# Four groups of tiles instead of three, the first of a single tile, and four whole chunks instead of eight

## The chip, the cores and the metric

The kernel runs on one core of a Trainium2 chip. The metric is device time in microseconds (us) of one execution. Inputs and outputs lie in the chip's main memory; the engines are TensorE (matmul, PE in the rows), VectorE (DVE), ScalarE (ACT), GpSimd (POOL) and SyncE (SP, which here only issues transfers).

## The reference, cut to what matters

One layer of an encoder over 1024 prompt tokens and 64 sample tokens (which also see 512 cached positions). Two attention branches, a gated merge, and then a layer of experts, each a single neuron, chosen per token by product keys:

```python
h = rmsnorm(x, norm_mix);  z = h @ w_in          # 1024 -> 5536 columns
# branch A: differential attention, 8 heads; branch B: latent attention, 16 heads
merged = gates[:, :, 0] * (o_a @ w_branch_a) + gates[:, :, 1] * (o_b @ w_branch_b)
x = x + merged @ w_out
x = x + peer_ffn(rmsnorm(x, norm_ffn), ...)      # then a last rmsnorm

def peer_tokens(h, w_q, keys, u, v):             # 8 heads, 16 experts of 16384 each
    q = (h @ w_q).reshape(T, 8, 2, 64)
    s = einsum('thcd,hcnd->thcn', q, keys)
    ...                                          # two top-16, 256 candidates, top-16 again
    act = gelu(einsum('td,thkd->thk', h, u[idx]))
    return einsum('thk,thkd->td', g * act, v[idx])
```

All values are fp32. Attention is causal by chunks of 64, so a tile of 128 prompt tokens with number t attends to t + 1 tiles of keys.

## The kernel before, in words

The 1088 tokens are nine tiles: 0 to 7 of 128 prompt tokens, and 8 with the 64 sample tokens. `GROUPS` says which tiles go through the layer together; there are three groups of three. The loop over groups (line 576) does, for its tiles: norm and transposes; the projections by `w_in`; the difference attention; `w_a`; the latent attention (MLA); a unit is one head of one tile, 24 in the first attention of a group and 48 in the second; `w_b`, `w_out`, a second norm, `w_pq`, and the expert scores. Every group reads all weights again, in chunks of 1024 rows by 256 columns (1 MB). A *token-major* chunk (`tmajor`) has the tokens of one tile as the stationary operand and streams the 256 columns, 8 products a tile. A *channel-major* one (`cmajor`) has the weights as the stationary operand, two halves of 128 columns, and streams all tokens of the group (`NH` columns), 16 products whatever their width. Of 38 chunks 14 are token-major (`w_in` 0 to 9, `w_out`) and 24 channel-major.

The first group is not native: each fp32 operand is split into a high and a low part, and a product is three matmuls (`mm3`, lines 153 to 155). ScalarE makes the high part of a weight chunk and GpSimd the low one (`wload`, lines 178 and 179). Later groups are native: one fp32 product (line 167), which leaves two records.

After a group's scores, three kinds of background work are queued for each tile and are let into the instruction streams by `pump`, in a proportion that `spread` works out from the planned units of work and the dots left:

- `route_job` (queue r): the top-16 searches, on VectorE (lines 470 to 560).
- `dots_job` (queue d): 128 gathers of rows of `peer_u` by GpSimd's queue (line 333), one expert for each token of the tile, each with a dot product on VectorE (line 358); 64 gathers for the sample tile, which packs two experts. In the first part seven buffers hold gathered rows (four `gb`, three `gm`), in the passes the four `gb`.
- `build_job` (queue b): makes the tile's matrix of weights by expert from one-hot matrices on VectorE (lines 402, 403, 411), ScalarE (line 408) and small bf16 matmuls (line 418), and stores it in `Ad`.

So a group's gathers run beside the next group, and those of the last group beside the passes. The passes multiply the matrices by all of `peer_v`, 16 chunks of 1024 rows: pass 0 for tiles 0, 1, 2, pass 1 for 3, 4, 5, 6. The first `NWHOLE` chunks of pass 0 are whole fp32 (line 1206), all others split in three (line 1221), for which ScalarE and VectorE make high and low parts of `peer_v` (lines 1190, 1192) and of the matrix (1214, 1215). Tile 6 (`TR`) keeps part of its matrix in a buffer `Ares` that exists only from the passes on. The tiles of `VGATHER`, 7 and 8, have no matrix: `vgather_job` gathers rows of `peer_v` and adds them up with weights on VectorE (line 453).

A scheduler puts the recorded instructions of each engine into one fixed order; each engine then runs its own in that order and waits on semaphores.

Of the kernel before, what the change touches and what calls it, by code (L numbers as in the profile page):

```python
# [31 lines left out]
LAMBDA_INIT = 0.8 - 0.6 * math.exp(-0.3 * 0)  # L32
MAGIC = float(0x5F3759DF)
MSC = 96.0 ** -0.5
GROUPS = ((0, 1, 2), (3, 4, 5), (6, 7, 8))
PASSES = ((0, 1, 2), (3, 4, 5, 6))
VGATHER = (8, 7)
GN = 384
SLOT = 3072
NW = 3  # L40
# [1 line left out]
PB = 5  # L42
NB = 8
RC = 9
NWHOLE = 8
TR = 6
RATE_R2 = 0.41
RATE_B, RATE_B2 = 0.3, 0.5
PUMP_G = (1.1, 1.113, 1.158)
RATE_R_G = (0.7, 0.7, 0.623)  # L50
DEPTH_DIFF = (3, 2, 2)
DEPTH_MLA = (2, 2, 2)


def bcast_rows(ap1d, n):
# [4 lines left out]
def hybrid_tile(ctx: ExitStack, tc: tile.TileContext, A):  # L60
# [16 lines left out]
    neard = dram("neard", (H, 128, 2, 256), F32R)  # L77
    gateT = dram("gateT", (len(GROUPS), 16, 128, GN), F32)
    sd = dram("sd", (9, 128, 2, H, 128), F32)
# [34 lines left out]
    cur = {"gp": gp, "sm": sm, "ps": ps_mm, "more": None}  # L114
# [181 lines left out]
    def spread(units, dots):  # L296
        left["units"], left["dots"] = units, left["dots"] + dots
# [41 lines left out]
    def dots_job(t):  # L339
        if t in GROUPS[-1]:  # L340
            drain("r", ("route", t))
# [21 lines left out]
        ld(wgtd[t, :, :ns], wgt[:, :ns])  # L363
        if t not in VGATHER:
            queues["b"].append((("build", t), build_job(t)))

    def build_job(t):
        if t == TR:
            drain("r")
        src = bp.tile([128, 3, 128], F32, name="bsrc", tag="oh1")  # L370
        ld(src[:, 0, :], wgtd[t])
        ld(src[:, 1:3, :], efd[t])
        p = cur["ps"].tile([128, 512], F32, name="mm")
        pv = p.rearrange("p (a n) -> p a n", n=128)
        for i in range(3):
            PE.transpose(pv[:, i, :], src[:, i, :], ident)
        ixT = bp.tile([128, 2, 128], BF16, name="ixT")
        S.copy(ixT, pv[:, 1:3, :])
        aT = bp.tile([128, 128], F32, name="aT")
        S.copy(aT, pv[:, 0, :])  # L380
        a3 = bp.tile([128, 3, 128], BF16, name="a3")
        a3f = bp.tile([128, 128], F32, name="a3f")
        for i in range(3):
            V.tensor_copy(a3[:, i], aT)
            if i == 0:
                V.tensor_copy(a3f, a3[:, 0])
            if i < 2:
                V.tensor_tensor(aT, aT, a3[:, i], op=ALU.subtract)
        yield
        shp = [128, 4, 128, 2]  # L390
        iv = iota2[:, None, :, :].to_broadcast(shp)

        def over(row, tt):
            return row[:, tt:tt + 8].rearrange("p (g x) -> p g x", x=2)[:, :, None, :].to_broadcast(shp)

        n = RC if t == TR else 0
        for t0 in range(0, 128, 16):
            stage = bp.tile([128, 16, 4, 8, 4], F32, name="stage", tag="stage")
            for tt in range(t0, t0 + 16, 8):
                oh1 = bp.tile(shp, BF16, name="oh1", tag="oh1")  # L400
                oh2 = bp.tile(shp, BF16, name="oh2")
                V.tensor_tensor(oh1, iv, over(ixT[:, 1], tt), op=ALU.is_equal)  # L402
                V.tensor_tensor(oh2, iv, over(ixT[:, 0], tt), op=ALU.is_equal)  # L403
                w3 = bp.tile([128, 3] + shp[1:], BF16, name="w3")
                for i in range(3):
                    if i == 0:
                        for x in range(8):
                            S.activation(w3[:, 0, x // 2, :, x % 2], oh2[:, x // 2, :, x % 2], AF.Copy,  # L408
                                         scale=a3f[:, tt + x:tt + x + 1])
                    else:  # L410
                        V.tensor_tensor(w3[:, i], oh2, over(a3[:, i], tt), op=ALU.mult)
                for q in range(2):
                    p = cur["ps"].tile([128, 512], F32, name="mm")
                    pv = p.rearrange("p (a n) -> p a n", n=128)
                    for j in range(4):
                        x = 4 * q + j
                        for i in range(3):
                            PE.matmul(pv[:, j, :], lhsT=oh1[:, x // 2, :, x % 2], rhs=w3[:, i, x // 2, :, x % 2],  # L418
                                      start=i == 0, stop=i == 2)
                    pc = p.rearrange("p (t c i) -> p c i t", t=4, i=8)  # L420
                    if n:
                        S.copy(cur["Ares"][:, :, (tt + 4 * q) // 4], pc[:, :n])
                    if n < 16:
                        S.copy(stage[:, n:, (tt - t0) // 4 + q], pc[:, n:])
                    yield
            ld(Ad[t, :, n:, t0 // 4:t0 // 4 + 4], stage[:, n:])

    def finish(acc, nr, t):
        if t in VGATHER:
            y = gp.tile([128, D], F32, name="y", tag="gb")  # L430
# [5 lines left out]
    def vgather_job(t):  # L436
# [18 lines left out]
        if t == 8:  # L455
            oth = cur["gp"].tile([128, D], F32, name="gb", tag="gb")
            ld(oth[0:64], acc[64:128])
            V.tensor_tensor(acc[0:64], acc[0:64], oth[0:64], op=ALU.add)
        if t == VGATHER[-1]:
            cur["late"] = lambda: finish(acc, tr(t), t)  # L460
# [3 lines left out]
    def route_job(t, s_of):  # L464
# [100 lines left out]
        ld(gkd[t, :nr], gk[:nr].rearrange("p h k -> p (h k)"))  # L565
        if t not in VGATHER:
            queues["d"].append((("dots", t), dots_job(t)))
        elif t not in GROUPS[-1]:
            queues["d"].append((("dots", t), dots_job(t)))
        if t == max(x for x in GROUPS[-1] if x < 8):  # L570
            for v in [x for x in VGATHER if x in GROUPS[-1]]:
                queues["d"].append((("dots", v), dots_job(v)))
            for v in VGATHER:
                queues["d"].append((("vg", v), vgather_job(v)))

    for g, tiles in enumerate(GROUPS):
        cur["g"] = g
# [4 lines left out]
        if g:  # L582
            nbs = [t + 1 if t < 8 else 5 for t in tiles]
            spread(2.6 * 14 * len(tiles) + 3.9 * 2 * 24 + (H + MH) * sum(PUMP_G[g] * (1 + n * 0.5) for n in nbs),
                   128 * len(GROUPS[g - 1]))
# [189 lines left out]
        def diff_unit(t, h, Q, qc, K, Vt, nr_, L):  # L775
# [58 lines left out]
            pend.append(fin)  # L834
            flush(DEPTH_DIFF[g])

# [303 lines left out]
    Ares = p2.tile([128, RC, 32, 8, 4], F32, name="Ares", bufs=1)  # L1140
# [11 lines left out]
    cur["rp"], cur["rs"] = rpt, rst  # L1152
    cur["Ares"] = Ares
    rate["r"], rate["b"] = RATE_R2, RATE_B2
    spread(16 * 8 * 1.3 * sum(len(x) for x in PASSES), sum((128 if t < 8 else 64) for t in GROUPS[-1] + VGATHER))
    gfin = p2.tile([128, D], F32, name="gfin", bufs=1)
    ld(gfin, bcast_rows(A["norm_final"], D))
    cur["gfin"] = gfin
# [7 lines left out]
    for ip, tiles in enumerate(PASSES):  # L1166
# [11 lines left out]
        for c in range(16):  # L1178
            vb = []
            whole = ip == 0 and c < NWHOLE  # L1180
            for i in range(8):
# [12 lines left out]
            for t in tiles:  # L1194
# [21 lines left out]
                if t in pst:  # L1216
                    for i in range(8):
                        for L, R in ((ahi, vb[i][0]), (ahi, vb[i][1]), (alo, vb[i][0])):
                            for hf in range(2):
                                ds = slice(512 * hf, 512 * hf + 512)  # L1220
                                PE.matmul(pst[t][:, ds], lhsT=L[:, i, :], rhs=R[:, ds],  # L1221
                                          start=c == (0 if ip else NWHOLE and -1) and i == 0 and L is ahi and R is vb[i][0],
                                          stop=c == 15 and i == 7 and L is alo)
# [114 lines left out]
```

## Time and profile before

| | |
|---|---|
| runs, median of 3 | 4505.98 us (4502.06 to 4518.71) |
| profiled execution, whole | 4499.18 us |
| its span, first to last instruction | 4497.4 us |
| TensorE busy | 3847.6 us, 86% |
| VectorE busy | 3203.9 us, 71% |
| GpSimd busy | 1942.8 us, 43% |
| ScalarE busy | 1603.3 us, 36% |
| moved by DMA | 1183.10 MB, 263 GB/s on average |
| granted TensorE clock, mean | 0.892 |

A busy TensorE is not one at its peak: a record's length holds the pipeline, so the distance between the starts of neighbouring matmuls is the better price. The mean shares hide stages with different limits; the span is to be read by stages.

### The profile page before, as it was taken

To read this page: it belongs to the slowest core of one execution; us is meant where nothing else is said; L and a number is where in the kernel's file an instruction comes from. 1 tells how busy PE (TensorE), PEld (TensorE's weight loads), DVE (VectorE), ACT (ScalarE), POOL (GpSimd) and SP (SyncE) were. 2 spreads that over 40 slices of the span, in tenths; PEclk is the share of its full clock that TensorE was granted. 3 is DMA by queue.
4 is the path that set the end of the run, shared out by engine and by line. 5 is a ranking of instruction groups with operands and counts; after the bars stand their busy time and mean duration, and the time that the engine had idled before them with its cause. 6 is when DMAs were issued, how large, how long until landed. Compare 5 with 4: busy or idle time off the path is not lost.

```text
span 4497.4 us, 55226 instructions
## 1 busy us (share of the span) xinstructions
PE 3847.6 (86%) x18633; PEld 2898.2 (64%) x18633; DVE 3203.9 (71%) x7136; ACT 1603.3 (36%) x3656; POOL 1942.8 (43%) x1353
## 2 busy tenths in 40 slices
PE   6998988898788798887868877889999969999991
PEld 6977887556565565655546666654457858888881
DVE  4043457977788767797786777659847987777776
ACT  3344622025455513322454455133113532232320
POOL 3412241554456441143444656513434445545455
PEclk9967999987898898998778888989999979999995
DMA  5421244996777785697776767988868999989987
GB/s 176 168 96 56 67 170 169 352 350 231 267 263 269 272 320 216 226 329 290 245 248 239 256 239 253 351 291 311 320 246 317 349 328 332 351 312 352 321 314 260
DMA packets 467587, 1183.10 MB, mean 263 GB/s; under 512 B 45352, under 2 KB 218888, under 8 KB 452584
## 3 DMA queue, kind: packets, MB, share of 16 engines
q0 software_dynamic: 184320, 671.17, 41.4%
q1 hardware_dynamic: 282984, 508.41, 32.3%
q8 instruction: 147, 2.41, 0.2%
q14 instruction: 136, 1.11, 0.1%
HBM read 1074.60 MB, written 104.56 MB: 262 GB/s over the span
## 4 chain that ended last, share of the span: by engine, by line
PE 42%; DMA 13%; DVE 13%; issue 5%; ACT 4%; POOL 2%; SPq 0%; another core or an unknown queue 0%; ACTq 0%; POOLq 0%; DVEq 0%
PE acc_ps L1221 16%; PE mm L167 9%; PE acc_ps L1206 5%; DMA Ad<-stage 4%; DMA gb<-in_peer_v,beidx 3%; DVE gb L358 3%; DMA gb<-in_peer_u,beidx 2%; PE mm L418 2%; DVE gm L358 2%; POOL gb L333 2%; PE mm L827 2%; PE sc L795 1%; PE mm L952 1%; PE sc L793 1%; ACT w L408 1%
## 5 line engine op out<-in xcount | busy, mean ns | idle before, releaser
L333 POOL DMA_INDIRECT gb<-in_peer_u,beidx x758 | 1028.2, 1356 | 1364.7 <-DVE gb L358 811.1
L358 DVE SCALAR_TENSOR_TENSOR gb<-gb,h2r 128x1024 f32<-128x1024 f32 x758 | 918.3, 1220 | 174.4 <-DMA gb<-in_peer_u,beidx 157.9
L333 POOL DMA_INDIRECT gm<-in_peer_u,beidx x330 | 429.9, 1303 | 501.4 <-DVE gm L358 274.6
L1221 PE MATMUL acc_ps<-vhi,ahi 128*128 128x512 f32 x1408 | 439.9, 395 | 23.4 <-ACT ahi L1214 23.4
L1221 PE MATMUL acc_ps<-vhi,alo 128*128 128x512 f32 x1408 | 444.1, 396 | 3.0 <-DVE alo L1215 3.0
L1221 PE MATMUL acc_ps<-vlo,ahi 128*128 128x512 f32 x1408 | 441.0, 395 | 0.0
L358 DVE SCALAR_TENSOR_TENSOR gm<-gm,h2r 128x1024 f32<-128x1024 f32 x330 | 402.1, 1218 | 24.0 <-DMA gm<-in_peer_u,beidx 21.4
L333 POOL DMA_INDIRECT gb<-in_peer_v,beidx x192 | 268.0, 1396 | 229.7 <-DVE gacc L453 150.1
L167 PE MATMUL mm<-h,wraw 128*128 128x384 f32 (+1 forms) x1024 | 325.5, 479 | 20.4 <-ACT qd L739 10.4
L1206 PE MATMUL acc_ps<-vw,aw 128*128 128x512 f32 x768 | 335.0, 596 | 1.4 <-ACT aw L1202 1.4
L418 PE MATMUL mm<-w,oh 128*128 128x128 bf16 x2688 | 231.0, 237 | 111.5 <-DVE oh L402 50.5
L1221 PEld LDWEIGHTS acc_ps<-vhi,ahi 128*128 128x128 f32 x1408 | 265.6, 189 | 85.5 <-ACT ahi L1214 23.6
L453 DVE SCALAR_TENSOR_TENSOR gacc<-gb,vwgt,gacc 128x1024 f32<-128x1024 f32 x192 | 246.2, 1282 | 93.3 <-DMA gb<-in_peer_v,beidx 88.1
L1221 PEld LDWEIGHTS acc_ps<-vhi,alo 128*128 128x128 f32 x1408 | 265.0, 189 | 63.9 <-DVE alo L1215 3.7
L1221 PEld LDWEIGHTS acc_ps<-vlo,ahi 128*128 128x128 f32 x1408 | 265.5, 189 | 60.2 <-DVE vlo L1192 0.2
L408 ACT ACTIVATE w<-oh,a3f 128x128 bf16<-128x128 bf16 x896 | 280.8, 429 | 54.0 <-DVE oh L403 24.3
L179 POOL TENSOR_TENSOR wlo<-wraw,whi 128x2048 fp32r<-128x2048 f32 (+1 forms) x42 | 186.8, 4447 | 260.6 <-ACT whi L178 255.0
L418 PEld LDWEIGHTS <-oh 128*128 128x128 bf16 x2688 | 191.9, 106 | 160.6 <-issue 73.2
L167 PEld LDWEIGHTS mm<-h,wraw 128*128 128x128 f32 x1024 | 201.0, 199 | 133.8 <-issue 11.4
L167 PE MATMUL mm<-wraw,h 128*128 128x256 f32 (+1 forms) x960 | 235.6, 402 | 37.7 <-ACT vt L720 27.8
L1206 PEld LDWEIGHTS acc_ps<-vw,aw 128*128 128x128 f32 x768 | 145.5, 191 | 179.1 <-issue 175.6
L1214 ACT CAST ahi<-araw 128x1024 fp32r<-128x1024 f32 x79 | 82.8, 1049 | 474.4 <-PE acc_ps L1221 395.7
(384 smaller groups left out, 7574.2 us busy)
## 6 DMA issues: line engine op xcount, KB each, us to landing
vraw<-in_peer_v SPq DMA_DIRECT2D x192, 512.0 KB
wraw<-in_w_in SPq DMA_DIRECT2D x66, 1024.0 KB
araw<-Ad SPq DMA_DIRECT2D x103, 512.0 KB
Ad<-stage SPq DMA_DIRECT2D x48, 1024.0 KB
vw<-in_peer_v SPq DMA_DIRECT2D x64, 512.0 KB
wraw<-in_w_a SPq DMA_DIRECT2D x12, 1024.0 KB
wraw<-in_w_b SPq DMA_DIRECT2D x12, 1024.0 KB
wraw<-in_w_out SPq DMA_DIRECT2D x12, 1024.0 KB
```

The source lines that it names most:

```text
L167: PE.matmul(out, lhsT=L[0], rhs=R[0], start=start, stop=stop)
L179: G.tensor_tensor(lo[:, :n], raw[:, :n], hi[:, :n].bitcast(F32), op=ALU.subtract)
L333: G.indirect_dma_start(out=gb, out_offset=None, in_=src, in_offset=bass.IndirectOffsetOnAxis(ap=idx, axis=0))
L358: behind(V.scalar_tensor_tensor(gb, gb, 1.0, h2, op0=ALU.mult, op1=ALU.mult, accum_out=act[:, k:k + 1]))
L408: S.activation(w3[:, 0, x // 2, :, x % 2], oh2[:, x // 2, :, x % 2], AF.Copy, scale=a3f[:, tt + x:tt + x + 1])
L418: PE.matmul(pv[:, j, :], lhsT=oh1[:, x // 2, :, x % 2], rhs=w3[:, i, x // 2, :, x % 2], start=i == 0, stop=i == 2)
L453: behind(V.scalar_tensor_tensor(acc, gb, wgt[:, k:k + 1], acc, op0=ALU.mult, op1=ALU.add))
L793: PE.matmul(ps[:nq, a:b], lhsT=Q[:, c, qc:qc + nq], rhs=K[:, c, a - o:b - o], start=True, stop=False)
L827: PE.matmul(po[:nq, :128], lhsT=PT[:kw, b, :nq], rhs=Vt[:kw, b, :], start=b == 0, stop=b == nb - 1)
L1206: PE.matmul(pst[t][:, ds], lhsT=rv[:, i, :], rhs=vb[i][:, ds], start=c == 0 and i == 0, stop=False)
L1214: S.copy(av, rv)
L1221: PE.matmul(pst[t][:, ds], lhsT=L[:, i, :], rhs=R[:, ds], start=c == (0 if ip else NWHOLE and -1) and i == 0 and L is ahi and R is vb[i][0 ...
```

## The change

`GROUPS` becomes (0), (1, 2, 3), (4, 5, 6), (7, 8): four groups, the weights read four times, and only tile 0 computed with split products, tiles 1 and 2 with native ones. The pump's constants get a fourth entry. Pass 0 has four whole chunks instead of eight. Of the two tiles without a matrix, 7 now comes ahead of 8. Tile 6 is no longer in the last group, so its build, which writes into `Ares`, waits with a loop until the passes have begun. In the passes the planned units that `spread` divides the dots by are taken times 0.93.

```diff
-GROUPS = ((0, 1, 2), (3, 4, 5), (6, 7, 8))
+GROUPS = ((0,), (1, 2, 3), (4, 5, 6), (7, 8))
 PASSES = ((0, 1, 2), (3, 4, 5, 6))
-VGATHER = (8, 7)
+VGATHER = (7, 8)
...
-NWHOLE = 8
+NWHOLE = 4
...
-PUMP_G = (1.1, 1.113, 1.158)
-RATE_R_G = (0.7, 0.7, 0.623)
-DEPTH_DIFF = (3, 2, 2)
-DEPTH_MLA = (2, 2, 2)
+PUMP_G = (1.1, 1.11, 1.13, 1.158)
+RATE_R_G = (0.7, 0.7, 0.7, 0.623)
+DEPTH_DIFF = (3, 2, 2, 2)
+DEPTH_MLA = (2, 2, 2, 2)
...
     def build_job(t):
+        while t == TR and "Ares" not in cur:
+            yield
         if t == TR:
...
-    spread(16 * 8 * 1.3 * sum(len(x) for x in PASSES), sum((128 if t < 8 else 64) for t in GROUPS[-1] + VGATHER))
+    spread(0.93 * 16 * 8 * 1.3 * sum(len(x) for x in PASSES), sum((128 if t < 8 else 64) for t in GROUPS[-1] + VGATHER))
```

The dots that stand in each group's part of VectorE's order: 384 in group 1 and 384 in group 2 before; 128 in group 1, 384 in group 2 and 384 in group 3 of the change. Behind the last group 320 dots and 192 weighted sums are left before, 192 and 192 in the change. Lines below `build_job` stand two lines lower in the changed kernel.

VectorE in the latent attention of the last group. A row with `nm<-sc` is the maximum of one unit's scores, on which its softmax waits; a row of line 358 is one dot product; the `oh` and `w` rows belong to a build. Before, with tiles 6, 7 and 8:

```order
L943 TENSOR_REDUCE nm_19509<-sc_19496 64x1
L358 SCALAR_TENSOR_TENSOR gb_19535,act_17261<-gb_19535,h2r_17257 128x1024
L358 SCALAR_TENSOR_TENSOR gm_19538,act_17261<-gm_19538,h2r_17257 128x1024
L358 SCALAR_TENSOR_TENSOR gb_19541,act_17261<-gb_19541,h2r_17257 128x1024
L1042 TENSOR_TENSOR ob_18556<-mm_19492,rb_19490 128x320
L943 TENSOR_REDUCE nm_19554<-sc_19544 128x1
L358 SCALAR_TENSOR_TENSOR gm_19581,act_17261<-gm_19581,h2r_17257 128x1024
L358 SCALAR_TENSOR_TENSOR gb_19584,act_17261<-gb_19584,h2r_17257 128x1024
L358 SCALAR_TENSOR_TENSOR gb_19587,act_17261<-gb_19587,h2r_17257 128x1024
L358 SCALAR_TENSOR_TENSOR gm_19590,act_17261<-gm_19590,h2r_17257 128x1024
L943 TENSOR_REDUCE nm_19615<-sc_19605 128x1
```

The same place in the change, with tiles 7 and 8:

```order
L945 TENSOR_REDUCE nm_21960<-sc_21950 128x1
L358 SCALAR_TENSOR_TENSOR gm_21988,act_20064<-gm_21988,h2r_20060 128x1024
L358 SCALAR_TENSOR_TENSOR gb_21991,act_20064<-gb_21991,h2r_20060 128x1024
L358 SCALAR_TENSOR_TENSOR gb_21994,act_20064<-gb_21994,h2r_20060 128x1024
L358 SCALAR_TENSOR_TENSOR gm_21997,act_20064<-gm_21997,h2r_20060 128x1024
L358 SCALAR_TENSOR_TENSOR gb_22000,act_20064<-gb_22000,h2r_20060 128x1024
L945 TENSOR_REDUCE nm_22080<-sc_22067 64x1
L358 SCALAR_TENSOR_TENSOR gm_22101,act_20064<-gm_22101,h2r_20060 128x1024
L358 SCALAR_TENSOR_TENSOR gb_22104,act_20064<-gb_22104,h2r_20060 128x1024
L404 TENSOR_TENSOR oh1_22017<-iota2_100,ixT_20075 128x1024
```

Three or four dots stood between two units' maxima; now five, or two and a build. Over this phase the order has 142 dots between 48 units' first and last maxima before, and 122 between 32 now.

The end of VectorE's order. `gacc` is the sum over gathered rows of `peer_v`, `araw<-acc_ps` takes a tile's sum out of the passes, the `rs` rows are a norm. Before:

```order
L197 SCALAR_TENSOR_TENSOR rs_y<-rs_t,rs_y 128x1
L205 SCALAR_TENSOR_TENSOR y<-araw,rs_y,gfin 128x1024
L453 SCALAR_TENSOR_TENSOR gacc<-gb,vwgt,gacc 128x1024 x8
L190 TENSOR_SCALAR rs_v<-rn_ss 128x1
L191 TENSOR_SCALAR rs_t<-rs_v 128x1
```

In the change:

```order
L205 SCALAR_TENSOR_TENSOR y<-araw,rs_y,gfin 128x1024
L1240 TENSOR_TENSOR araw<-acc_ps,araw 128x1024
L190 TENSOR_SCALAR rs_v<-rn_ss 128x1
L191 TENSOR_SCALAR rs_t<-rs_v 128x1
L192 TENSOR_SCALAR rs_y<-rs_t 128x1
```

Weighted sums used to stand behind the last tile's norm; in the change none stands behind the first of the last tiles' norms.

## Rows read from the trace of the kernel before

**Rows 1.** The page's first lines: span, and busy time of each engine.

```profile
span 4497.4 us, 55226 instructions
PE 3847.6 (86%) x18633; PEld 2898.2 (64%) x18633; DVE 3203.9 (71%) x7136; ACT 1603.3 (36%) x3656; POOL 1942.8 (43%) x1353
```

**Rows 2.** Stages: from:to, length; PE, PEld, DVE, ACT, POOL busy; clock, DMA, GB/s.

```profile
0.00:233.00 233.00, 184.86 (x1227) 181.38 (x1228) 61.33 (x186) 78.19 (x118) 92.71 (x25) 0.95 0.51 172
233.00:419.00 186.00, 165.65 (x711) 138.72 (x709) 73.06 (x157) 77.30 (x233) 39.49 (x12) 0.71 0.25 83
419.00:548.00 129.00, 124.36 (x725) 99.60 (x725) 53.57 (x115) 91.25 (x286) 29.86 (x19) 0.96 0.11 37
548.00:704.00 156.00, 139.90 (x865) 130.66 (x864) 90.64 (x311) 49.42 (x76) 54.64 (x18) 0.93 0.45 157
704.00:968.00 264.00, 226.52 (x827) 158.61 (x826) 225.48 (x867) 37.06 (x86) 114.57 (x96) 0.94 0.84 311
968.00:1255.00 287.00, 231.76 (x1064) 161.29 (x1063) 220.66 (x399) 137.67 (x370) 119.10 (x94) 0.79 0.76 262
1255.00:1590.00 335.00, 269.64 (x1660) 204.44 (x1659) 272.37 (x470) 182.04 (x491) 183.46 (x137) 0.87 0.76 259
...
1757.00:2089.00 332.00, 262.84 (x1289) 192.28 (x1289) 272.73 (x1060) 98.89 (x271) 101.03 (x86) 0.88 0.74 263
2089.00:2425.00 336.00, 261.25 (x1227) 179.41 (x1226) 248.99 (x437) 159.93 (x417) 131.25 (x95) 0.80 0.73 249
2425.00:2823.00 398.00, 322.88 (x2099) 258.24 (x2098) 303.27 (x510) 201.59 (x537) 235.43 (x152) 0.85 0.71 240
2823.00:2990.00 167.00, 144.19 (x629) 106.33 (x627) 98.57 (x208) 29.51 (x66) 67.01 (x51) 0.86 0.91 339
2990.00:3347.00 357.00, 351.88 (x1078) 165.12 (x1079) 265.00 (x991) 79.84 (x167) 109.87 (x91) 0.99 0.80 284
3347.00:3690.00 343.00, 302.08 (x1552) 242.59 (x1551) 284.79 (x427) 154.36 (x293) 155.70 (x111) 0.93 0.92 335
3690.00:4400.00 710.00, 709.46 (x3063) 575.95 (x3061) 552.29 (x610) 193.29 (x188) 386.90 (x274) 1.00 0.90 330
4400.00:4497.00 97.00, 0.00 (x0) 0.00 (x0) 66.44 (x103) 4.59 (x8) 49.20 (x39) 0.52 0.75 255
```

**Rows 3.** Timeline of TensorE in group 0's projections: start, length, instruction.

```profile
153.91 0.28 PE L155 MATMUL mm<-whi,hlo 128*128 128x256 f32 x1
154.03 0.34 PE L153 MATMUL mm<-hhi,whi 128*128 128x384 f32 x1
154.21 0.33 PE L154 MATMUL mm<-hlo,whi 128*128 128x384 f32 x1
```

**Rows 4.** The same view in group 0's MLA scores.

```profile
421.64 0.41 PE L154 MATMUL sc<-CK,ql 128*128 128x128 f32 x1
421.85 0.41 PE L155 MATMUL sc<-CK,ql 128*128 128x128 f32 x1
...
423.70 0.41 PE L154 MATMUL sc<-CK,ql 128*128 128x256 f32 x1
423.91 0.41 PE L155 MATMUL sc<-CK,ql 128*128 128x256 f32 x1
```

**Rows 5.** The chain in group 1's native projections: start, length, records.

```profile
962.00 5.16 PE mm L167 x16
```

**Rows 6.** The page's groups: one dot product; busy, mean ns, idle before.

```profile
L358 DVE SCALAR_TENSOR_TENSOR gb<-gb,h2r 128x1024 f32<-128x1024 f32 x758 | 918.3, 1220 | 174.4 <-DMA gb<-in_peer_u,beidx 157.9
```

**Rows 7.** The chain in pass 1.

```profile
3687.37 487.44 PE acc_ps L1221 x2096
```

**Rows 8.** The page's groups: the low part of a weight chunk, on GpSimd.

```profile
L179 POOL TENSOR_TENSOR wlo<-wraw,whi 128x2048 fp32r<-128x2048 f32 (+1 forms) x42 | 186.8, 4447 | 260.6 <-ACT whi L178 255.0
```

**Rows 9.** Groups by line: a routing step, and the maximum of a unit's scores.

```profile
L471 DVE FIND_INDEX8 idx<-vals,sc 128x8 uint32<-128x128 f32 x48 | 13.1, 285 | 0.0
L943 DVE TENSOR_REDUCE nm<-sc 128x1 f32<-128x128 f32 (+2 forms) x144 | 108.1, 752 | 68.5 <-PE sc L941 56.3 <-ACT rb L1037 5.5 <-ACT Pm L945 3.1
```

## The prediction, made blind

> **What bounds the kernel now.** The line of busy times comes first [rows 1]: TensorE 86%, VectorE 71%, and no engine full. So the time is not one engine's sum, and the view that counts is the second: busy times by stage [rows 2], cut at the first and last instruction of each phase. It shows four regimes. In group 0 (0 to 704 us) TensorE works, VectorE is about 40% busy and DMA at most half: no gathers run, since no expert is chosen yet. In groups 1 and 2 (704 to 2990) the gathers for the group before fill the phases: TensorE and VectorE are both near 80% and neither gets much further, because each softmax goes back and forth between them and its steps stand in VectorE's queue behind dot products. The passes (2990 to 4400) are TensorE alone, 99 to 100%, but for 41 us where pass 0 hands over to pass 1 (343 us with 302 busy). The last 97 us are gathers of `peer_v` for one tile, with TensorE idle. So the tail and the light VectorE of group 0 can be gained; a fourth group is what is paid.
>
> **Unit prices.** A split matmul starts every 0.12 us at 256 columns and every 0.18 at 384 [rows 3]. At 128 columns it is no cheaper than at 256: in the MLA scores those of 128 columns stand 0.21 us apart, and so do those of 256 beside them [rows 4] (both at a lowered clock). So I price 128 columns at 0.12. A native matmul leaves two records: 16 records, 8 matmuls of 384 columns, in 5.16 us [rows 5] is 0.645 us each, and in proportion 0.43 at 256. A dot product is 1.22 us [rows 6]. In pass 1, 2096 records in 487.44 us [rows 7] make 0.698 us for the three of a split product.
>
> **The change, part by part.**
>
> *A fourth set of weights.* Each group runs 14 token-major chunks (8 products of 256 columns a tile) and 24 channel-major ones (16 products as wide as the group), and four for MLA. The channel-major cost goes by groups more than by tokens; that is the price.
>
> *Group 0, (0).* A token-major chunk takes TensorE 24 x 0.12 = 2.9 us, but GpSimd's low part takes 4.45 a chunk [rows 8], so GpSimd sets the pace: 4.45. A channel-major chunk is 48 x 0.12 = 5.8 us. Before, both were 8.6. Against rows 2: to 233 us there were 18 chunks, 155 us, and 78 us of start and stalls; now 10 x 4.45 + 8 x 5.8 + about 50 = 140. From 233 to 419: eight channel-major chunks, 69 us, and 117 of attention; now 46 + 45 = 91 (a third of 117 is 39, but keys and values are still loaded once a head). MLA, 129: a third is 43, but the preparation by pair of heads doesn't shrink with it; 55. From 548 to 704: 103 us of chunks and 53 of chains; now 64 + 20 = 84. Sum 370 us; 320 if the chains hide, 430 if stalls don't shrink with tiles.
>
> *Group 1, (1, 2, 3).* Chunks cost 10.3 us of TensorE each, as in group 1 before, and it has 128 dots, not 384. Projections were 264 with TensorE 227 busy: 250. Difference attention lies between group 0's 186 and group 1's 287 (keys of 2 to 4 tiles, 28 dots): 215. MLA between 129 and 335: 175. The end as in the other groups, 167. Sum 807 (740 to 860).
>
> *Group 2, (4, 5, 6).* 384 dots, three routed tiles and three builds, as in group 2 before, with key lengths between those of groups 1 and 2. Its projections hold 462 routing rows, 59 of build and 87 dots in the order, against 462, 59 and 79 in group 2 before, which took 332: 325. Then 300 (of 287 and 336), 365 (of 335 and 398), 167. Sum 1157 (1090 to 1220).
>
> *Group 3, (7, 8).* TensorE has two thirds of a group's work here, but the gathers, routing and builds of three tiles must fit beside it. The order puts 57, 122 and 138 dots into its phases, against 79, 95 and 154 in the last group before: 3.8 dots a unit of MLA instead of 3. From VectorE's 273, 249 and 303 us of group 2 [rows 2], with 92 routing rows of about 0.28 us [rows 9] moved from the first phase to the second, and a third of the reductions gone (8 units of two, 16 of one, 0.75 us each [rows 9]), I get 273 - 27 - 26 = 220, 249 + 33 + 26 - 12 = 296, 303 - 20 - 12 = 271 (dots at 1.22). VectorE's best share in a phase with gathers is 85% (225 of 264); the attention phases had 74 to 81%. With less TensorE work between, I take 85% throughout: 259 + 348 + 319, and 120 for the end (167 with fewer tiles). Sum 1046. At 92% it is 960 (with 105), at 75% 1179 (with 130).
>
> The groups then take 370 + 807 + 1157 + 1046 = 3380 us, against 2990.
>
> *Passes.* Eight whole chunks took 357 us; four take 180. The other eight took 302 busy us, 268 of them their own (48 x 0.698 = 33.5 each), so 34 for 384 build matmuls. Twelve take 402, 26 for the 288 builds that the order leaves there, and about 20 for the handover, since tile 6's dots, which pass 1 needs, are done by then: 448. The four chunks made split save TensorE about 30 us (41 whole against 33.5) and cost VectorE 4 x 11 x 1.22 = 54 us of low parts; they are hidden by TensorE in a stage where VectorE was 83% busy, which has 128 dots fewer. Uncovered they would cost those 54. Pass 1 stays at 710. Together 1338, against 1410.
>
> *Tail.* 512 dots and weighted sums stood after the last group, now 384, and the end of VectorE's order holds no weighted sum, only the norms of the last tiles: 15 us for 97 (12 to 40).
>
> Sum: 3380 + 1338 + 15 = 4733 us of span, against 4497.4 [rows 1]. The profiled execution took 4499.18 us, 2 more, and the median of the runs is 4505.98. I forecast **4735 us**, 5% slower: 390 us for the groups against 154 won behind them.
>
> [...]
>
> **The rivals.** *Faster, 4432 us.* What groups 1 and 2 lose before is coupling, and it may shrink when dots have more time: group 0 at 320, group 1 at 740, group 2 at 1090, group 3 with VectorE at 92%, 960, the passes 1305, the tail 15, and 2. It decides once groups and passes take 252 us less than I sum. For it: 704 to 968 us has VectorE at 85% and TensorE at 86% together. Against it: no attention phase passes 81%. Chance 8%.
>
> [...] Chance 12%.
>
> *The fourth group hides, 4505.* Only TensorE's extra work counts: channel-major chunks 24 x (5.8 + 10.3 + 10.3 + 5.2) against 24 x (8.6 + 10.3 + 8.6), 98 us, some 16 for two tiles made native, 30 less in pass 0, and the tail pays for it. For it: TensorE has the highest share. Against it: in the groups its idle time is chains, which regrouping doesn't shorten. Chance 6%.
>
> *The tail stays, 4817.* If the weighted sums of tiles 7 and 8 still run after pass 1, because four gather buffers are too few while DMA is 90% busy [rows 2], 82 us come back. Against it: the order has 153 sums within pass 1 before, and 192 need little more. Chance 6%.
>
> **How the numbers follow.** The forecast has 68%, its own range 4610 to 4850. All bounds taken together would give 4432 and 5090, which I don't expect at once. The range for 8 in 10 is 4560 to 4870. About 0.5%, 23 us, is what a measurement can tell here from no change. Faster by more (under 4483): 9%, the first rival and a little of the third; within: 6%; slower: 85%.
>
> **What would show it.** Group 0 should end near 370 us, group 1 near 1180, group 2 near 2330, group 3 near 3380, and TensorE's last matmul some 15 us before the end. In group 3's attention VectorE should be above 80% busy and TensorE below 70%. A group 3 under 950 us would prove me wrong on the main term; so would a group 0 under 310.

## The result, and the profile after

The changed kernel takes **4906.26 us** (median of 4 runs, 4890.59 to 4917.4) against 4508.71 for the kernel before: a ratio of 1.0877, 95% interval 1.0839 to 1.0915. That is 8.8% slower, where 4735 us (5%) was forecast; the time lies 36 us above the forecast range. The profiled execution has a span of 4915.6 us. Lines below `build_job` stand two lines lower than in the rows of before.

The page's first lines, answering [rows 1]: span, and busy time of each engine.

```profile
span 4915.6 us, 57721 instructions
...
PE 4122.4 (84%) x19497; PEld 3183.7 (65%) x19497; DVE 3245.9 (66%) x7304; ACT 1676.3 (34%) x3828; POOL 1976.9 (40%) x1351
```

TensorE is busy 275 us longer with 864 more records, VectorE 42 us longer; the span is 418 us longer, and the shares of both fell (86 to 84%, 71 to 66%). The stages, answering [rows 2], with the same columns (from:to, length; PE, PEld, DVE, ACT, POOL busy; clock, DMA share, GB/s). Each group has four rows: projections, difference attention, MLA, end. Group 0 is the first four rows, group 1 the next four, and so on; then come the whole chunks, the rest of pass 0, pass 1 and the tail.

```profile
0.00:206.00 206.00, 149.70 (x775) 145.83 (x775) 34.72 (x86) 62.13 (x84) 100.23 (x26) 0.66 0.46 162
206.00:314.00 108.00, 91.48 (x390) 84.90 (x389) 26.72 (x87) 32.16 (x94) 26.19 (x8) 0.50 0.28 89
314.00:384.00 70.00, 68.06 (x283) 60.01 (x283) 22.15 (x81) 38.66 (x140) 21.53 (x19) 0.50 0.18 59
384.00:518.00 134.00, 119.23 (x570) 114.86 (x570) 58.44 (x185) 34.73 (x49) 48.91 (x18) 0.58 0.41 145
518.00:772.00 254.00, 218.85 (x831) 158.13 (x830) 92.39 (x344) 35.62 (x90) 55.64 (x44) 0.92 0.61 216
772.00:958.00 186.00, 157.31 (x622) 105.16 (x620) 96.20 (x195) 78.14 (x233) 28.28 (x28) 0.87 0.53 173
958.00:1115.00 157.00, 147.37 (x815) 105.75 (x815) 99.96 (x188) 94.70 (x273) 39.20 (x37) 1.00 0.46 146
1115.00:1268.00 153.00, 139.27 (x555) 96.35 (x555) 69.75 (x234) 21.31 (x39) 20.37 (x19) 0.95 0.62 224
1268.00:1598.00 330.00, 273.79 (x1288) 199.11 (x1288) 279.16 (x1059) 100.38 (x267) 121.76 (x94) 0.90 0.78 278
1598.00:1952.00 354.00, 284.46 (x1193) 195.08 (x1192) 233.44 (x406) 147.14 (x380) 121.94 (x92) 0.73 0.62 210
1952.00:2305.00 353.00, 289.46 (x1878) 229.59 (x1879) 285.07 (x481) 197.78 (x515) 198.27 (x143) 0.89 0.76 256
2305.00:2469.00 164.00, 150.41 (x616) 105.86 (x614) 116.17 (x324) 26.48 (x53) 69.00 (x55) 0.93 0.86 327
2469.00:2728.00 259.00, 193.38 (x1143) 161.16 (x1143) 218.10 (x865) 87.15 (x250) 77.00 (x65) 0.86 0.80 286
2728.00:3055.00 327.00, 195.63 (x887) 139.49 (x887) 258.61 (x517) 122.15 (x329) 168.72 (x121) 0.66 0.83 289
3055.00:3386.00 331.00, 232.50 (x1465) 190.83 (x1464) 244.87 (x435) 142.95 (x398) 196.01 (x134) 0.75 0.73 249
3386.00:3564.00 178.00, 110.19 (x632) 93.32 (x629) 111.30 (x220) 36.14 (x89) 87.62 (x64) 0.78 0.96 360
3564.00:3757.00 193.00, 177.64 (x484) 82.34 (x485) 160.32 (x634) 39.15 (x81) 70.10 (x51) 0.95 0.75 262
3757.00:4216.00 459.00, 436.37 (x2087) 352.95 (x2086) 355.21 (x501) 184.95 (x279) 200.19 (x137) 0.97 0.89 328
4216.00:4904.00 688.00, 687.31 (x3003) 563.02 (x3001) 477.44 (x452) 192.41 (x190) 325.92 (x196) 1.00 0.79 286
4904.00:4916.00 12.00, 0.00 (x0) 0.00 (x0) 5.90 (x29) 2.19 (x4) 0.00 (x0) 0.57 0.21 66
```

Put against the forecast, stage by stage:

| stage | forecast | measured | difference |
|---|---|---|---|
| group 0 | 140 + 91 + 55 + 84 = 370 | 206 + 108 + 70 + 134 = 518 | +148 |
| group 1 | 250 + 215 + 175 + 167 = 807 | 254 + 186 + 157 + 153 = 750 | -57 |
| group 2 | 325 + 300 + 365 + 167 = 1157 | 330 + 354 + 353 + 164 = 1201 | +44 |
| group 3 | 259 + 348 + 319 + 120 = 1046 | 259 + 327 + 331 + 178 = 1095 | +49 |
| whole chunks, rest of pass 0, pass 1 | 180 + 448 + 710 = 1338 | 193 + 459 + 688 = 1340 | +2 |
| tail | 15 | 12 | -3 |
| sum | 4733 | 4916 | +183 |

One row carries 148 of the 183: group 0. There the granted clock is 0.66, 0.50, 0.50 and 0.58, while every stage of groups 1 to 3 but two is at 0.75 or more. Inside its projections, in shorter windows (the same columns):

```profile
80.00:100.00 20.00, 13.45 (x79) 13.05 (x79) 0.00 (x0) 5.00 (x6) 13.21 (x3) 0.68 0.43 156
100.00:106.00 6.00, 4.89 (x44) 4.75 (x43) 0.00 (x0) 4.55 (x4) 4.29 (x1) 1.00 0.68 218
120.00:140.00 20.00, 20.00 (x96) 20.00 (x95) 0.00 (x0) 4.71 (x6) 8.57 (x3) 0.50 0.34 106
```

From 80 to 100 us, in token-major chunks with waits between them, TensorE is two thirds busy at 0.68. At the end of the last of them, dense from 94.16 us and at 0.50 until 99.17, the clock rises to the upper of the two levels that it shows here (1.00), and the first channel-major chunk behind it runs there. TensorE then waits 1.43 us for GpSimd's low part, and just behind that wait, at about 106.5 us, the clock falls to the lower level (0.50). There it stays through the channel-major chunks that follow (0.50 from 106.5 to 206 us); from 120 to 140 us TensorE has no idle time at all. Matmuls of both levels on TensorE's timeline (start, length, instruction):

```profile
100.04 0.27 PE L155 MATMUL mm<-hhi,wlo 128*128 128x128 f32 x1
100.15 0.27 PE L153 MATMUL mm<-hhi,whi 128*128 128x128 f32 x1
...
106.32 0.33 PE L155 MATMUL mm<-hhi,wlo 128*128 128x128 f32 x1 [1.43 <-POOL wlo L179]
...
119.88 0.41 PE L153 MATMUL mm<-hhi,whi 128*128 128x128 f32 x1
120.09 0.41 PE L154 MATMUL mm<-hlo,whi 128*128 128x128 f32 x1
```

In the first chunk they start 0.11 us apart, and 48 of them take 5.4 us (99.17 to 104.61): for this one chunk the forecast's 5.8 was near. In the later ones they start 0.21 us apart, so a chunk of 48 takes 10.2 us. GpSimd's timeline shows the same pace from the other side: one low part per chunk, with GpSimd idle 5.72 us before each.

```profile
128.32 4.52 POOL L179 TENSOR_TENSOR wlo<-wraw,whi 128x2048 fp32r<-128x2048 f32 x1 [5.72 <-ACT whi L178]
138.56 4.52 POOL L179 TENSOR_TENSOR wlo<-wraw,whi 128x2048 fp32r<-128x2048 f32 x1 [5.72 <-ACT whi L178]
```

The starts are 10.24 us apart. So what one of these chunks costs is TensorE's 128-column matmuls at the lower clock (0.50), and nothing feeds them late.

### The profile page after: what moved, and what is told of

Same layout as the page of the kernel before. It is cut to its first block, busy times and chain, and to the rows that moved or that the text cites. A ratio compares the mean times of both kernels' runs of the same rounds, so it can differ in the third digit from the quotient of the medians.

```text
span 4915.6 us, 57721 instructions
## 1 busy us (share of the span) xinstructions
PE 4122.4 (84%) x19497; PEld 3183.7 (65%) x19497; DVE 3245.9 (66%) x7304; ACT 1676.3 (34%) x3828; POOL 1976.9 (40%) x1351
## 4 chain that ended last, share of the span: by engine, by line
PE 61%; DVE 15%; DMA 15%; issue 4%; ACT 4%; POOL 1%; SPq 0%; ACTq 0%; DVEq 0%; POOLq 0%
PE acc_ps L1223 21%; PE mm L167 18%; DMA Ad<-stage 7%; DVE gb L358 4%; DVE gm L358 2%; PE mm L954 2%; PE mm L153 2%; PE mm L154 2%; PE mm L155 2%; PE mm L420 2%; PE sc L797 2%; DMA gb<-in_peer_u,beidx 1%; PE tp L760 1%; PE mm L829 1%; PE sc L795 1%
## 5 line engine op out<-in xcount | busy, mean ns | idle before, releaser
L333 POOL DMA_INDIRECT gb<-in_peer_u,beidx x704 | 948.8, 1348 | 1406.3 <-DVE gb L358 924.5
L358 DVE SCALAR_TENSOR_TENSOR gb<-gb,h2r 128x1024 f32<-128x1024 f32 x704 | 850.8, 1219 | 99.6 <-DMA gb<-in_peer_u,beidx 78.0
L333 POOL DMA_INDIRECT gm<-in_peer_u,beidx x384 | 509.8, 1328 | 875.9 <-DVE gm L358 489.2
L358 DVE SCALAR_TENSOR_TENSOR gm<-gm,h2r 128x1024 f32<-128x1024 f32 x384 | 468.0, 1219 | 40.4 <-DMA gm<-in_peer_u,beidx 39.3
L167 PE MATMUL mm<-h,wraw 128*128 128x384 f32 (+1 forms) x1536 | 452.1, 456 | 37.4 <-ACT stage L426 27.5
L167 PEld LDWEIGHTS mm<-h,wraw 128*128 128x128 f32 x1536 | 295.7, 203 | 178.8 <-ACT stage L426 32.3
L167 PE MATMUL mm<-wraw,h 128*128 128x256 f32 (+1 forms) x1280 | 312.9, 402 | 63.5 <-ACT vt L722 36.4
L167 PEld LDWEIGHTS mm<-wraw,h 128*128 128x128 f32 (+1 forms) x1280 | 244.2, 195 | 113.6 <-ACT vt L722 38.3
L1192 ACT CAST vhi<-vraw 128x1024 fp32r<-128x1024 f32 x224 | 234.4, 1052 | 114.2 <-PE acc_ps L1223 62.7
L1194 DVE TENSOR_TENSOR vlo<-vraw,vhi 128x1024 fp32r<-128x1024 f32 x224 | 266.1, 1218 | 4.9 <-ACT vhi L1192 3.7
```

What stands on the lines that cost most here:

```text
L167: PE.matmul(out, lhsT=L[0], rhs=R[0], start=start, stop=stop)
L333: G.indirect_dma_start(out=gb, out_offset=None, in_=src, in_offset=bass.IndirectOffsetOnAxis(ap=idx, axis=0))
L358: behind(V.scalar_tensor_tensor(gb, gb, 1.0, h2, op0=ALU.mult, op1=ALU.mult, accum_out=act[:, k:k + 1]))
L1192: S.copy(hi, raw)
L1194: V.tensor_tensor(lo, raw, hi.bitcast(F32), op=ALU.subtract)
```

## The experiments

All ratios are to the kernel before.

### Is group 0 slow because its products are 128 columns wide?

**Group 0 padded to 256 columns.** The channel-major products of group 0 stream the tile twice, side by side:

```diff
+        NC = max(NH, 256) if g == 0 else NH
...
+                if nk == 8 and NC > NH:
+                    put(pv[:, :kn, :nr], [x[:, k0:k0 + kn, NH:NC] for x in X], scale)
...
-                mmx(p[:, :NH], [x[:, k, sl] for x in w], [x[:, k, :NH] for x in X], k == 0, k == 7)
+                mmx(p[:, :NC], [x[:, k, sl] for x in w], [x[:, k, :NC] for x in X], k == 0, k == 7)
...
```

> The changed kernel, but in the single-tile group every channel-major product streams 256 columns instead of 128: the tile's 128 columns and a copy of them, whose results are not read. TensorE's work in these 24 chunks doubles in columns. Theory width (dense matmuls of 128 columns do not raise the granted clock from 0.50, those of 256 do, as in group 0 before): the stretch of the gate chunks runs at 0.9 or more, a chunk takes 5.8 us instead of 10.2, group 0 ends about 105 us sooner, less some 10 us for the copies: near 420 us instead of 518, and the kernel near 4810. Theory gaps (the clock fell because token-major chunks wait for GpSimd's low parts, and stays where it fell): the clock stays at 0.50, a 256-column matmul starts every 0.21 us, a chunk still takes 10.2 us, and the kernel stays within 15 us of 4906.

Measured: 4833.36 us, ratio 1.0717 (1.0688 to 1.0745), 73 us less than the changed kernel. Group 0 ends at 424 us instead of 518, where the first of the two theories expected 420. A window of its channel-major chunks and its MLA, the columns as before:

```profile
120.00:140.00 20.00, 19.29 (x162) 19.08 (x162) 0.00 (x0) 7.21 (x10) 14.86 (x4) 1.00 0.57 196
...
250.00:328.00 78.00, 75.10 (x309) 65.97 (x309) 23.50 (x86) 41.76 (x153) 26.26 (x29) 0.50 0.19 60
```

And its channel-major matmuls on TensorE's timeline:

```profile
124.45 0.28 PE L155 MATMUL mm<-hhi,wlo 128*128 128x256 f32 x1
124.57 0.28 PE L153 MATMUL mm<-hhi,whi 128*128 128x256 f32 x1
```

Twice the columns, 0.12 us apart instead of 0.21: 48 of them take 5.7 us, the price that the prediction had put on 128 columns. In the window from 120 to 140 us the clock is 1.00 and TensorE 19.29 of 20 us busy. The padding is pure extra work and saves 94 us in group 0; 21 of them come back in group 1, whose length goes from 754 to 775 us between the last score matmuls of the two groups, and the rest of the span moves by under 10 us (one profile of each kernel). MLA, which was not padded, stays at 0.50.

**Group 0 native.** One fp32 product in place of three split ones, still 128 columns wide:

```diff
-        nat = cur["native"] = g > 0
+        nat = cur["native"] = True
```

(The tile `cq` of group 0 then comes from another pool; the rest is the same.)

> The changed kernel with the single-tile group native as the others: one fp32 product instead of three split ones, no high and low parts on ScalarE and GpSimd. Theory width, if what counts is the columns of one matmul: 128-column products stay at clock 0.50, a channel-major chunk takes 16 x 0.43 = 6.9 us against 10.2, token-major ones are limited by their loads; group 0 ends 80 to 110 us sooner (410 to 440), the kernel near 4810. [...] Theory gaps: without GpSimd in the chain the token-major gaps go, and the clock rises too; the padded run tells the two apart.

Measured: 4714.34 us, ratio 1.046 (1.0435 to 1.0485), 192 us less than the changed kernel. Group 0 ends at 307 us, over 100 less than the theory of width expected (410 to 440, the kernel near 4810). Its four stages:

```profile
0.00:103.00 103.00, 74.64 (x452) 66.63 (x453) 17.54 (x73) 18.61 (x50) 0.20 (x4) 0.97 0.83 291
103.00:175.00 72.00, 56.89 (x362) 50.31 (x360) 24.45 (x93) 24.79 (x99) 0.00 (x0) 0.76 0.53 178
175.00:242.00 67.00, 65.31 (x258) 53.50 (x258) 22.49 (x83) 30.45 (x129) 0.00 (x0) 0.52 0.21 69
242.00:307.00 65.00, 56.17 (x379) 51.32 (x378) 26.31 (x141) 12.28 (x28) 0.00 (x0) 0.91 0.81 289
```

A run of its records on the timeline:

```profile
85.79 7.51 PE L167 MATMUL mm<-h,wraw 128*128 128x128 f32 x63
```

63 records of 128 columns in 7.51 us are 0.119 each, in a stage at 0.97, where split ones of the same width take 0.21 at 0.50. But native records do not always stand at the upper level: in the MLA of this run, at 0.52 with TensorE busy for 65 of 67 us, there are native ones of line 167, also 128 columns wide, among the 258.

Shown is this: behind 106.5 us the dense stream of split 128-column matmuls stayed at the lower level, and with padding alone (1.00 from 120 to 140 us), or with native products in the same chunks (1.00 from 80 to 100 us), the clock was at the upper one. So most of what group 0 lost (94 of 148 us, by the padded run) comes from the clock, and not from late operands. What lets it fall after the first chunk, the 1.43 us of waiting or the chunk itself, and what keeps it down were not varied by themselves and stay open.

How busy TensorE is in the profile does not tell the level here. In the token-major chunks the clock rose in a dense stretch: behind a wait of 6.37 us the last of them starts at 0.50, and at its end the clock is 1.00. In the dense channel-major stream it didn't: TensorE is busy for 20.00 of 20 us, and the clock stays at 0.50.

### What does the fourth set of weights cost?

**Two tiles in the first two groups.**

```diff
-GROUPS = ((0,), (1, 2, 3), (4, 5, 6), (7, 8))
+GROUPS = ((0, 1), (2, 3), (4, 5, 6), (7, 8))
```

> The changed kernel with groups (0, 1), (2, 3), (4, 5, 6), (7, 8): still four sets of weights, but the first group has 256 columns, and 256 dots instead of 128 stand beside the second, 256 instead of 384 beside the third. If the clock of the single tile is the main loss, group 0 is near 430 us at a clock of 0.9 (against 518 for one tile at 0.56), group 1 near 560 (752 for three native tiles), group 2 near 1120: the kernel near 4560, still above the kernel before, whose groups need one set of weights less. If a fourth set of weights is the loss and the clock is not, group 0 takes longer than 518 us and the sum of groups 0 and 1 stays near 1270: the kernel near 4850.

Measured: 4735.17 us, ratio 1.0499 (1.047 to 1.0527). The time lies between the two cases of the expectation, 175 us above the first. Group 0 takes 500 us, for two tiles 18 less than for the one of the changed kernel, with clocks of 0.93, 0.70, 0.90 and 0.92. But group 1, with tiles 2 and 3, takes 698 us where 560 were expected. Two of its stages:

```profile
695.00:876.00 181.00, 124.44 (x457) 92.62 (x455) 142.49 (x278) 62.61 (x178) 99.57 (x80) 0.68 0.90 317
...
1051.00:1198.00 147.00, 112.49 (x560) 94.93 (x560) 100.05 (x247) 22.12 (x53) 70.34 (x58) 0.87 0.97 367
```

TensorE is 69% busy in the first and 77% in the second, with DMA at 0.90 and 0.97. We read this as 256 dots, with their gathers and routing, not fitting beside two tiles; no run varied it. The balance with much of the clock's cost gone: four groups are 229 us slower than three in this form, and 208 with group 0 native. Some of the clock's cost is left in both (0.68 in the first stage above, 0.52 in the native MLA of 67 us).

**Group 3 with half of its dots.** The dots and gathers of tiles 4, 5 and 6 are cut from 128 to 64 each, and the number that `spread` plans with follows.

```diff
-        for k in range(ns):
+        if t in (4, 5, 6):
+            V.memset(act[:, 64:], 0.0)
+        for k in range(64 if t in (4, 5, 6) else ns):
...
-                   128 * len(GROUPS[g - 1]))
+                   (64 if g == 3 else 128) * len(GROUPS[g - 1]))
```

> The changed kernel with half of the dot products left out for tiles 4, 5 and 6 (64 gathers and dots a tile instead of 128; the other 64 weights come out as zero), so 192 dots instead of 384 stand beside the last group (7, 8). If VectorE's queue sets that group's time, as forecast, it takes about 192 x 1.22 = 234 us less, 200 at a share of 0.85: near 890 us instead of 1095, and the kernel near 4700. If the group is set by TensorE at a lowered clock and by its chains, it loses less than 100 us: the kernel above 4800.

**Group 3 with all dots and half of the gathers.** Every second gather of these tiles is left out, and its dot runs on the row that is already there.

```diff
-            gb = gather(A["peer_u"], eidx[:, k:k + 1])
+            if not (t in (4, 5, 6) and k % 2):
+                gb = gather(A["peer_u"], eidx[:, k:k + 1])
```

> The changed kernel, but for tiles 4, 5 and 6 every second gather is left out and its dot product runs a second time on the row gathered before (so those dots have wrong values): VectorE's and the order's 384 dots beside group (7, 8) stay, with 192 gathers of 0.5 MB, 100 MB less. The run with half of the dots had both halved and took 227 us off that group. If VectorE's queue was the cause, group (7, 8) stays within 40 us of its 1095 us and the kernel above 4850. If the transfers were, it falls by 150 us or more, the kernel to 4750 or below.

Measured, one run each: 4687.96 and 4862.16 us. Group 3 with half of the dots:

```profile
2465.00:2679.00 214.00, 156.71 (x994) 128.67 (x993) 175.47 (x672) 79.36 (x227) 60.89 (x50) 0.88 0.81 278
2679.00:2929.00 250.00, 195.35 (x990) 143.97 (x988) 192.19 (x494) 124.19 (x339) 71.92 (x47) 0.75 0.73 246
2929.00:3165.00 236.00, 197.89 (x1420) 162.22 (x1421) 159.09 (x286) 134.70 (x382) 87.14 (x62) 0.88 0.57 188
3165.00:3333.00 168.00, 117.38 (x725) 101.17 (x722) 88.01 (x182) 49.73 (x135) 50.17 (x34) 0.81 0.85 294
```

And with half of the gathers alone:

```profile
2474.00:2730.00 256.00, 175.97 (x1020) 144.72 (x1020) 224.08 (x759) 81.21 (x231) 69.34 (x50) 0.81 0.70 231
2730.00:3033.00 303.00, 212.08 (x1014) 155.36 (x1013) 254.83 (x656) 127.12 (x348) 73.90 (x46) 0.71 0.62 206
3033.00:3313.00 280.00, 214.41 (x1368) 174.23 (x1365) 222.30 (x399) 133.89 (x369) 107.29 (x59) 0.80 0.48 152
3313.00:3501.00 188.00, 125.66 (x755) 107.49 (x756) 138.84 (x275) 50.67 (x137) 62.28 (x37) 0.80 0.79 272
```

With half of the dots group 3 takes 868 us instead of 1095, 227 less, and VectorE's busy time in it goes from 833 to 615, 218 less: nearly one for one, though VectorE is only 62 to 84% busy in the group. That is near the first case of its expectation (890). With all dots and half of the gathers it takes 1027, 68 less, with VectorE at 840: between the two cases of that expectation. If the two parts simply add, VectorE's dots are the larger one (about 160 of 227) and the gathers the smaller (about 70); a run with half of the dots and all gathers, which would test the sum, is missing. The fourth phase is 10 us shorter in the first run and 10 us longer in the second: neither explains why it is 178 us long.

### Four whole chunks or eight?

**The changed kernel with eight.** `NWHOLE = 4` becomes 8.

> The changed kernel with eight whole chunks again: only the other part of the change stays. By TensorE's prices pass 0 gets 4 x 7.6 = 30 us longer: 4936 against 4906. If VectorE's low parts (54 us more with four whole chunks) were uncovered, they would vanish here and the kernel would be the same or up to 25 us faster.

Measured: 4941.49 us, ratio 1.0982 (1.0948 to 1.1016), 35 us above the changed kernel by the medians and 47 by the ratios. In the profiles the 1352 us from the first whole chunk to the end become 1379; there four chunks are whole instead of split, in a stage that TensorE fills.

**The kernel before with four.** `NWHOLE = 8` becomes 4.

> The kernel before with four whole chunks instead of eight, nothing else. TensorE saves 30 us in pass 0, VectorE gets 54 us of low parts in a stage where it was 75 to 83% busy and had 512 dots and sums. If they are hidden: 30 us faster, near 4475. If VectorE's order is the limit there, the sums of the last tile move back and the tail grows by about as much: within 25 us of 4503, or slower by up to 54.

Measured: 4547.58 us, ratio 1.0093 (1.0065 to 1.0121), 0.9% slower. Its split chunks:

```profile
3192.00:4448.00 1256.00, 1165.06 (x5189) 939.88 (x5187) 972.41 (x1245) 396.62 (x526) 661.26 (x445) 0.95 0.89 322
```

From the first whole chunk to the end it takes 1544 us, where the kernel before takes 1507 [rows 2]; TensorE idles 91 us among the split chunks. The same edit gains with 384 dots and sums behind the last group and loses with 512. The two kernels also differ in the factor 0.93 and in which tiles are left then, so the number of dots is the likely reason and not a shown one. The tail stays (95 us), so the changed kernel's short tail does not come from this number.

**The kernel before with twelve whole chunks** (and the passes' planned units times 0.93):

> The kernel before with three groups, the pace of 0.93 and 12 whole chunks in pass 0 instead of 8. With four whole chunks the three-group kernel was 47 us slower, which puts the limit of its passes on VectorE. By that theory four more whole chunks cost TensorE 4 x 7.5 = 30 us and take 4 x 13.4 = 54 us of low parts from VectorE, so that VectorE's dots and sums end earlier: between 30 and 50 us of the tail of 97 go, and the time is 4490 or a little less (4470 to 4500). The rival is that TensorE sets the end of pass 1 whatever VectorE does, and the tail is set by the gathers' transfers: then the 30 us are added, 4520 to 4535.

Measured: 4505.86 us, ratio 0.9987 (0.997 to 1.0004): no change from the kernel before, and by the ratios 0.2% above the same pace with eight, with intervals that overlap. TensorE's last matmul moves from 4423 to 4438 us, the tail from 74 to 63. Neither expectation holds: about half of TensorE's 30 us is paid, and the tail gives back less than was hoped.

### Is there a better kernel with three groups?

The factor 0.93 of the change, and two smaller ones, alone in the kernel before:

```diff
-    spread(16 * 8 * 1.3 * sum(len(x) for x in PASSES), ...)
+    spread(0.93 * 16 * 8 * 1.3 * sum(len(x) for x in PASSES), ...)
```

> The kernel before with the planned units of the passes times 0.93, nothing else. 7% of 512 dots and sums, about 36, move from behind pass 1 into the passes; 39 sums took the 97 us of the tail. If TensorE stays as dense in the passes, the tail falls to 15 to 40 us and the kernel to about 4430 to 4450. If the earlier dots hold up the splitting of chunks, pass 0 grows by as much and the kernel stays near 4500.

> The kernel before with the planned units of the passes times 0.86 instead of 1 (0.93 gave 4491, the tail 74 us instead of 97 and TensorE's end 24 us later). Theory: dots and sums are only moved ahead, against TensorE's low parts, so each us of tail is paid by nearly one us of TensorE: 4480 to 4500, no more than 0.3% from the run with 0.93. The rival, that the tail was left there by the pace alone, expects another 15 to 25 us less: 4465 to 4475.

> The kernel before with the planned units of the passes times 0.78. The factors 1, 0.93 and 0.86 gave 4506, 4491 and 4477, 15 us for each step, so pulling dots and sums ahead has so far cost TensorE less than it took from the tail. Theory: the passes' start becomes VectorE's now, and what the tail still gives (some 60 us are left) is paid by TensorE's waits there: 4470 to 4490. The rival, that the line goes on, expects 4455 to 4465.

| factor | median us | ratio, interval | passes' first matmul | last matmul | tail |
|---|---|---|---|---|---|
| 1 (before) | 4505.98 | | 2990 | 4400 | 97 |
| 0.93 | 4491.42 | 0.9967 (0.9946 to 0.9988) | 3002 | 4423 | 74 |
| 0.86 | 4476.68 | 0.9927 (0.99 to 0.9954) | 3004 | 4405 | 78 |
| 0.78 | 4481.96 | 0.9955 (0.993 to 0.998) | 2990 | 4423 | 52 |

(Each ratio is to runs of the kernel before made beside it; the last three columns come from one profile of each.) With 0.86 the kernel is 0.7% faster than before, and 430 us below the changed one: the lowest median of this study.

With 0.78 the tail is shorter still, but the passes end as late as with 0.93. The intervals of 0.86 and 0.78 overlap, so the turn itself is not settled; no further gain is seen. With 0.86 the time fell between the two expectations, 3 us below the one and 2 above the other, and the theory that each microsecond of tail is paid by nearly one of TensorE does not hold there: 19 us of tail went for 5 us of TensorE's end. For 0.78 it fits again, since the passes end 18 us later than with 0.86 for 26 us of tail. But the passes' start moves by as much as 14 us between these profiles, so neither figure is settled.

## Why the prediction was wrong, point by point

**The step that failed: "So I price 128 columns at 0.12."** [Rows 4] showed 128 and 256 columns equally long, at the lower clock (0.50 from 421 to 424 us). The prediction carried the equality to the upper clock, and there it holds: the first channel-major chunk took 5.4 us. What failed is that it put all 24 chunks at the upper clock, without asking whether a dense stream of split 128-column matmuls keeps it. It didn't: from 106.5 us on it stood at 0.50 and took 0.21. That put group 0 at 370 us; it took 518. [Rows 2] showed dense chunks at 0.93, but those were 384 and 256 columns wide. The row was evidence about other widths, and no row of before had a dense stretch of 128-column split matmuls. What stood nearest were matmuls of 128 and 256 columns in group 0's difference attention, 0.71 on average; that row should have had the weight. Inside it a window of the kernel before shows the lower level with TensorE nearly always busy:

```profile
280.00:300.00 20.00, 18.86 (x62) 14.41 (x63) 9.47 (x23) 9.04 (x32) 0.00 (x0) 0.50 0.25 76
```

Priced at the 0.21 us of [rows 4], the 24 chunks of 48 matmuls come to 24 x 48 x 0.09 = 104 us more than at 0.12, by this estimate. With them group 0 is at 474 and the forecast at 4839, inside its range and 67 us from the measured time.

The padded run sizes this: 94 of the 148 us are in what the padding cured. The other 54, by the stages of that run (154, 96, 78 and 96 us), are 14, 5, 23 and 12 us. MLA is the largest: 78 us in the padded run at a clock of 0.50, where 55 were forecast and three tiles ran at 0.96 [rows 2].

**Group 1** was 57 us shorter than forecast, 29 in the difference attention and 18 in MLA. With 128 dots VectorE is 36 to 64% busy in it and TensorE 85 to 94%. We read this as the coupling that costs groups with 384 dots being mostly absent there, which no run varied; the prediction's faster rival had 740 for this group, and came near on it alone.

**Group 2** was 44 longer, more than all of it in the difference attention: 354 against 300, at a clock of 0.73. The forecast took it between the 287 and 336 us of before [rows 2], whose clocks were 0.79 and 0.80. Why the clock is lower there was not tried.

**Group 3**, the main term, was forecast at 259 + 348 + 319 and took 259 + 327 + 331: right in sum to 9 us. Two errors cancel in it. VectorE was busy 37 and 26 us less in the attention phases than worked out, and its share was 79% and 74%, not 85%, so the mark "above 80%" was missed there; TensorE's 60% and 70% came about as said, the second at its very edge. That VectorE's dots set most of the length fits the two runs with half of the dots and half of the gathers. The end was 58 us longer than the 120 put on it. The chain of waits shows there, with DMA at 0.96:

```profile
3415.54 0.59 ACT stage L426
3416.15 14.49 DMA Ad<-stage
3431.03 0.59 ACT stage L426
3431.66 1.44 PE mm L420 x12
3433.10 3.41 PE mm L167 x16
...
3441.35 13.97 DMA Ad<-stage
```

These two stores of a build's pieces take 14.49 and 13.97 us, and TensorE's next product (line 167) stands behind the small matmuls of that build (line 420). "167 with fewer tiles" priced TensorE's work and left out these waits. With half of the gathers, DMA's share in this phase was 0.79, but the phase was no shorter (188 us); VectorE had 139 us of work in it instead of 111. What would shorten it is open.

**The passes** were right: 193, 459 and 688 against 180, 448 and 710. That four whole chunks are better than eight here is shown by the run with eight (35 us by the medians, 30 were forecast). That it hangs on VectorE's 128 dots fewer fits the same edit in the kernel before, which costs 37 us in the profiles and 48 by the medians, near the forecast's "uncovered" 54; but those two kernels differ in more than the dots.

**The tail** is 12 us, 15 forecast. In the kernel before, neither four whole chunks (95 us) nor a smaller factor (52 us at least) brings it, so the regrouping is left, with the order of tiles 7 and 8; the two were not varied apart. The factor 0.93, which the prediction gave no term, is worth 0.3% by itself in the kernel before.

**The rivals.** That the fourth group hides (4505) is out: with group 0 native, below even the 320 us of the faster rival, the kernel is still 208 us over before. That the tail stays (4817) is out by the last row of the stages. The faster one (4432) came near on group 1 only.

## What to carry to other kernels

Before pricing a matmul narrower than any in the trace, ask at which clock its stream will run, and take the price of the lower level as an end of the range with a real chance: a busy TensorE in the profile does not say that it runs at its upper clock (20.00 of 20 us busy at 0.50, here). Where a narrow split product stays at the lower one, a native product or even padding with a copy can be cheaper, as both were here (3.8 and 5.7 us a chunk against 10.2). And cutting work into more groups costs more than one further set of weights: here the background work of three tiles also had to stand beside a group of only two, and in its first three phases that group took 917 us, where 926 were forecast.

## What the runs showed of the hardware that was not expected

- Dense split matmuls of 128 columns stood at a granted clock of 0.50 with TensorE busy for 20.00 of 20 us, 0.21 us apart; the same products padded to 256 columns ran at 1.00, 0.12 us apart, so that twice the columns took 56% of the time (5.7 against 10.2 us for 48). One chunk of 128 columns, the first, ran at 1.00 as well: 0.11 us apart, 5.4 us for 48.
- Native fp32 records of 128 columns took 0.119 us in a stage at 0.97, so a native channel-major chunk for one tile (32 records, 3.8 us) was cheaper than a split one at either clock (5.4 and 10.2 us). In MLA, where they stand among other matmuls, the clock was 0.52 all the same.
- VectorE at 62 to 84% busy still went far to set the length of a group: with half of the dots and gathers gone, 218 us less of its work went with 227 us less of time, of which the gathers alone, halved in another run, gave 68.
